# The second condition's norm sums, fifteen products further back in the tensor engine's order

## The chip, the cores and the metric

One core of a Trainium2 chip runs the whole program. The core has TensorE (PE, the matrix engine), VectorE (DVE), ScalarE (ACT), GpSimd (POOL) and SyncE (SP), which here only issues DMAs. Each engine works through its own queue in order; the engines meet at semaphores. The metric is the device time of one execution in microseconds, the median of the runs shown; less is better.

## The reference

The program is a small flow-matching trunk: two layers over 256 latent tokens, with 256 context tokens as a prefix, width 1024. Every layer is a half-step SwiGLU, a token mixer (an mLSTM in the first layer, windowed attention with sinks in the second), and another half-step SwiGLU. Each sub-layer's input is shifted and scaled by vectors made from a condition, and its output goes through a norm:

```python
def modulate(s, m, slot):
    return s * (1 + m[..., 3 * slot + 1, :]) + m[..., 3 * slot, :]

def residual_post_norm(s, y, gate, weight, g, b):
    return layer_norm(ALPHA * s + weight * gate * y, g, b)

for i in range(DEPTH):
    m_l = (lat_cond @ mod_w[i] + mod_b[i])      # condition of the latent tokens
    m_c = (ctx_cond @ mod_w[i] + mod_b[i])      # condition of the context tokens
    h  = residual_post_norm(h,  swiglu(modulate(h,  m_l, 0), ...), gate_of(m_l, 0), 0.5, ...)
    hc = residual_post_norm(hc, swiglu(modulate(hc, m_c, 0), ...), gate_of(m_c, 0), 0.5, ...)
    ...
```

Latent and context tokens share all weights and differ in the condition. The context's last sub-layers are not needed, so the last two norms have latent tokens alone.

## The kernel before

**Layout.** Activations lie with the 1024 features on eight blocks of 128 partitions (`as_[0]` to `as_[7]`, "d" or "t" below) and the 512 tokens in the free dimension. Columns 0 to 255 are the context (`C0`, "context half" below, the first condition), columns 256 to 511 the latent tokens (`C1`, "latent half", the second condition). Matrices are multiplied as sums of three products: each fp32 operand is split into a high part and a low part (h and l: uh, ul; hh, hl), and high x high, high x low and low x high are added. Weights arrive by DMA as `raw`, and are split by ACT (line 413) and DVE (line 414) into `w`.

**The planner.** PE's and SP's order is written by a planner. Every stage is a Python generator, a task; `drive` keeps a clock of estimated time, `k.T`, which every planned product advances, and always takes the due task of the best priority. A task that yields a number asks to be taken up again that many planned nanoseconds later. The table `LAT` on line 32 has five such delays, all used in the class `Norm`. The order of ACT, DVE and POOL is made afterwards by a scheduler that goes by its own estimates, so it can shift when PE's order does.

**A norm with two halves.** Four norms have both halves: behind the first SwiGLU, behind the mLSTM, and behind the next two SwiGLUs ("first" to "fourth norm" below). For each half, in this order:

- The last products of the sub-layer (`y`) end; DVE adds them to the residual (line 830) and the engines sum values and squares over the eight blocks (lines 99 to 108, tiles `acc`, `sq`).
- `Norm.finish` waits a planned delay, `LAT[0]` for the context half and `LAT[1]` for the latent half, and then puts the sums over the partitions into PE's queue: four products on columns and one of 128x256 into the tile `stat` (the profile counts two passes for each).
- ACT takes them out of PSUM (lines 166, 167, 170); POOL makes the inverse root (lines 168, 865 to 870, tile `ln`) and subtracts the mean (line 173, eight times).
- After `LAT[2]` two products spread the inverse root over the partitions (tile `rstd`).
- For each block DVE multiplies by it (line 197); the condition's scale and shift give the next stage's input: uh by ACT (line 624), uf and ul by DVE (lines 625 and 626). The tiles `A` and `B` of the norm are named cA or cB in the profile.
- POOL later scales the residual for the next norm (line 203); `L92` prepares the factors (`ag`) of such a scaling.

After `LAT[3]` or `LAT[4]` the next stage (`g_heads`) may plan its first products: for each half, eight blocks of 12 products of 128x256, so 96 per half (called `xm` before the mLSTM, `gv` before a SwiGLU, `k` and `v` before attention). The context half's 96 products stand in the queue while the latent half's norm is worked on, and the latent half's 96 follow.

```python
        yield LAT[0] if cs == s.halves[0] else LAT[1]      # line 156
        ...                                                # stat products, inverse root
        yield LAT[2]                                       # line 179
        yield from s.scale(cs, y)                          # rstd products, lines 197, 624 to 626
```

**Around the norms.** The conditions' matrices are worked through beside the main stages by `mods`: DMAs of `mraw`, products with a scalar on ACT (line 532) and DVE (line 534) into `macc`, then sums over the partitions (`msum`) and transposes (`mtp`) on PE. These tasks rest while a norm is near: `k.calm` opens `CALM` = 10,000 planned ns after the latent half's sums, and is closed again for `CM` = 80,000 ns when the mixer's first products have been planned (line 995, in `g_ml_main`). `split` gives weight splits another priority while `calm` is closed.

**Start of the mLSTM.** `g_ml_main` plans the `xm` products of the first four of 16 blocks for both halves, then the others with all 512 columns at once. Per block `g_tile` lets DVE copy xm out of PSUM (line 1057), convolve it (lines 1060 and 1061), split it (line 612, `xcl`), and plans products for `v`, `q` and the scores `S`. POOL issues stores of the residual (line 1000, `rs`) between its scalings.

Of the kernel before, what the change touches and what calls it, by code (L numbers as in the profile page):

```python
# [28 lines left out]
MLP, ZP, ATP, HNP, VP = (2,), (1, 3), (2,), (1,), (1, 3)  # L29


LAT = (1700, 3500, 3000, 2000, 2200)

SOLO, RY, ST, LT = 2000, 14000, 2500, 1500

# [37 lines left out]
class Norm:  # L73
# [75 lines left out]
    def finish(s, cs):  # L149
# [5 lines left out]
        k.res[cs.start] = Ev()  # L155
        yield LAT[0] if cs == s.halves[0] else LAT[1]

# [19 lines left out]
        if s.left == 0:  # L177
            k.free(s.a1, s.a2)
        yield LAT[2]
        yield from s.scale(cs, y)  # L180

    def scale(s, cs, y):
# [7 lines left out]
        c = 0 if cs == C1 else 1  # L190
        s.ready[cs.start].t = k.T + (LAT[3] if cs == s.halves[0] else LAT[4])
        y = bc[:, cs]
# [1436 lines left out]
```

## Time and profile before

| | |
|---|---|
| median of 3 runs | 1928.77 us (1927.26 to 1932.07) |
| profiled execution, device time | 1928.09 us |
| its span, first to last instruction | 1926.1 us, 27938 instructions |
| mean granted clock of PE | 0.986 |
| DMA | 287.48 MB, 149 GB/s in the mean |
| first norm: latent sums on PE at | 409.04 us |
| second norm | 835.56 us |
| third norm | 1210.85 us |
| fourth norm | 1586.27 us |

The profile has one execution. A row of the timeline gives the start, the time from the start of the first to the end of the last instruction in the row, engine, line, operation, tiles (written <- read), shape and count; in brackets stands the idle time of the engine before the row and what ended it. A row of the waits gives the sum of such idle times, their number and the longest. All of PE's products are issued by one helper, line 323 (transposes by line 330), so they are told apart by their tiles.

### The profile page before, as it was taken

How to read it: one execution, taken by the hardware profiler on the slowest of the kernel's cores; microseconds unless marked ns; L12 is line 12 of the kernel's file. 1: busy time of each engine (PE TensorE's matmuls, PEld its weight loads, DVE VectorE, ACT ScalarE, POOL GpSimd, SP SyncE). 2: the span in 40 equal slices, each digit the busy share in tenths (PEclk: the TensorE clock that was granted, in tenths of full speed). 3: DMA queues.
4: the chain of work that ended last, by engine and by line, in shares of the span. 5: the costliest groups of instructions: out<-in, count | busy, mean ns of one | idle time of the engine just before them, and what ended most of it. 6: DMA issues, size and time to landing. Idle time of an engine off the chain costs nothing.

```text
span 1926.1 us, 27938 instructions
## 1 busy us (share of the span) xinstructions
PE 1876.3 (97%) x10474; PEld 1587.1 (82%) x10474; DVE 1356.8 (70%) x2489; ACT 829.4 (43%) x1557; POOL 358.1 (19%) x384
## 2 busy tenths in 40 slices
PE   7999999999999999989999999999999999989997
PEld 4888888897879987988888889888888899788887
DVE  4976677976664689777775768877633468977675
ACT  3443233246645564343323333433223335747562
POOL 2000000470012344450000015500000246120000
PEclk9999999999999999989999999999999999999999
DMA  9665455426343464325455443354422323125652
GB/s 319 211 210 170 153 177 179 137 93 204 99 155 103 143 224 143 103 91 183 165 202 175 169 138 131 125 191 165 153 88 93 104 73 132 45 67 178 209 170 100
DMA packets 227432, 287.48 MB, mean 149 GB/s; under 512 B 7969, under 2 KB 197537, under 8 KB 227297
## 3 DMA queue, kind: packets, MB, share of 16 engines
q1 hardware_dynamic: 226384, 282.75, 44.1%
q0 software_dynamic: 912, 2.95, 0.4%
q8 instruction: 82, 1.34, 0.3%
q14 instruction: 54, 0.43, 0.1%
HBM read 269.94 MB, written 15.73 MB: 148 GB/s over the span
## 4 chain that ended last, share of the span: by engine, by line
PE 56%; DVE 3%; POOL 1%; issue 1%; ACT 0%; DVEq 0%; POOLq 0%
PE gv L323 31%; PE y L323 19%; PE q L323 1%; PE s L323 1%; PE o L323 1%; DVE ul L626 1%; PE pT L330 1%; PE stat L323 0%; DVE uf L625 0%; PE msum L323 0%; PE h L323 0%; DVE as L197 0%; POOL as L173 0%; ACT e L1457 0%; PE swap L323 0%
## 5 line engine op out<-in xcount | busy, mean ns | idle before, releaser
L323 PE MATMUL gv<-uh,w 128*128 128x512 f32 (+1 forms) x2240 | 670.3, 381 | 11.0 <-DVE w L414 5.5
L413 ACT ACTIVATE w<-raw 128x512 fp32r<-128x512 f32 x636 | 394.6, 629 | 656.1 <-PE gv L323 357.6
L414 DVE TENSOR_TENSOR w<-raw,w 128x512 fp32r<-128x512 f32 x604 | 432.5, 722 | 270.9 <-ACT w L413 266.1
L323 PEld LDWEIGHTS gv<-uh,w 128*128 128x128 f32 x2240 | 416.2, 190 | 97.3 <-DVE w L414 5.7
L323 PE MATMUL gv<-ul,w 128*128 128x512 f32 (+1 forms) x1120 | 424.5, 379 | 0.1
L534 DVE SCALAR_TENSOR_TENSOR macc<-mraw,cs,macc 128x512 f32<-128x512 f32 x448 | 330.6, 781 | 36.6 <-DMA mraw<-in_mod_w 26.4
L323 PE MATMUL y<-hh,w 128*128 128x512 f32 (+1 forms) x1248 | 340.8, 359 | 0.0
L323 PEld LDWEIGHTS y<-hh,w 128*128 128x128 f32 x1248 | 222.6, 189 | 37.8 <-issue 2.2
L323 PEld LDWEIGHTS gv<-ul,w 128*128 128x128 f32 x1120 | 212.8, 190 | 38.7 <-DVE ul L626 0.6
L323 PE MATMUL y<-hl,w 128*128 128x512 f32 (+1 forms) x624 | 222.4, 356 | 0.0
L88 POOL TENSOR_TENSOR as<-as,shift 128x512 f32<-128x512 f32 (+1 forms) x40 | 57.2, 1463 | 886.2 <-ACT shift L86 886.2
L323 PEld LDWEIGHTS y<-hl,w 128*128 128x128 f32 x624 | 117.9, 189 | 17.5 <-issue 0.7
L323 PE MATMUL gv<-up,w 128*128 128x256 f32 x704 | 124.2, 338 | 1.5 <-ACT up L624 1.2
L323 PEld LDWEIGHTS gv<-up,w 128*128 128x128 f32 x704 | 108.1, 190 | 17.5 <-ACT up L624 1.4
L830 DVE SCALAR_TENSOR_TENSOR as<-y,gate,as 128x256 f32<-128x256 f32 x192 | 82.0, 475 | 37.7 <-PE y L323 37.7
L323 PE MATMUL z<-w,uh 128*128 128x256 f32 x512 | 94.2, 285 | 0.0
L323 PE MATMUL xm<-uh,w 128*128 128x512 f32 (+1 forms) x320 | 91.7, 360 | 0.0
L323 PE MATMUL y<-hnh,w 128*128 128x512 f32 (+1 forms) x320 | 85.0, 350 | 0.0
L414 POOL TENSOR_TENSOR w<-raw,w 128x512 fp32r<-128x512 f32 x32 | 45.7, 1429 | 201.6 <-ACT w L413 193.6
L323 PEld LDWEIGHTS z<-w,uh 128*128 128x128 f32 x512 | 79.9, 192 | 2.5 <-issue 2.1
L743 DVE TENSOR_TENSOR sg<-sg,gv 128x512 f32<-128x512 f32 x66 | 44.9, 684 | 47.7 <-PE gv L323 46.3
L323 PE MATMUL z<-w,ul 128*128 128x256 f32 x256 | 72.4, 283 | 0.0
(318 smaller groups left out, 2519.8 us busy)
## 6 DMA issues: line engine op xcount, KB each, us to landing
raw<-in_ffn_w_in SPq DMA_DIRECT2D x84, 1024.0 KB, 5.2
mraw<-in_mod_w SPq DMA_DIRECT2D x128, 512.0 KB, 6.1
raw<-in_ffn_w_out SPq DMA_DIRECT2D x48, 768.0 KB, 4.6
raw<-in_ml_w_up SPq DMA_DIRECT2D x15, 1024.0 KB, 6.0
m<-in_mod_w SPq DMA_DIRECT2D x32, 256.0 KB, 6.6
raw<-in_ffn_w_out SPq DMA_DIRECT2D x16, 512.0 KB, 3.5
raw<-in_ml_w_down SPq DMA_DIRECT2D x16, 512.0 KB, 4.1
raw<-in_at_w_qkv SPq DMA_DIRECT2D x6, 1024.0 KB, 5.2
```

The costliest lines, as they stand in the source:

```text
L88: nc.gpsimd.tensor_tensor(out=k.as_[d][:, cols], in0=k.as_[d][:, cols], in1=sh[:, cols], op=ALU.subtract)
L323: k.nc.tensor.matmul(out, lhsT=lhsT, rhs=rhs, start=start, stop=stop, skip_group_check=True, **kw)
L330: k.nc.tensor.transpose(out, in_, k.ident[0:p, 0:p])
L413: k.nc.scalar.activation(h, view, AF.Copy)
L414: (k.nc.gpsimd if pool else k.nc.vector).tensor_tensor(out=l, in0=view, in1=h.bitcast(F32), op=ALU.subtract)
L534: V.scalar_tensor_tensor(out=o, in0=r, scalar=cf, in1=o, op0=ALU.mult, op1=ALU.add)
L626: nc.vector.tensor_tensor(out=lo, in0=f[:, cs], in1=hi.bitcast(F32), op=ALU.subtract)
L743: nc.vector.tensor_tensor(out=sg[:, cols], in0=sg[:, cols], in1=gv[1][:, cols], op=ALU.mult)
L830: nc.vector.scalar_tensor_tensor(out=k.as_[d][:, cs], in0=ys[dp][e][:, part], scalar=G[:, d, c:c + 1], in1=k.as_[d][:, cs], op0=ALU.mult, ...
```

## The change

One number of the planner's table: the latent half's sums are planned 5000 instead of 3500 planned ns after the half's last products.

```diff
-LAT = (1700, 3500, 3000, 2000, 2200)
+LAT = (1700, 5000, 3000, 2000, 2200)
```

No instruction is added or removed; their order changes. On PE, at the first norm, the latent half's sums leave their place in the third block's products (`uh_3477`) ...

```order
 L323 MATMUL xm<-ul_3478,w 128x256
-L323 MATMUL xm<-uh_3477,w 128x256
-L323 MATMUL stat<-ones_85,acc_2963 128x1 x2
-L323 MATMUL stat<-ones_85,acc_2964 128x1 x2
-L323 MATMUL stat<-acc_2963,ones_85 128x256
-L323 MATMUL xm<-uh_3477,w 128x256
+L323 MATMUL xm<-uh_3477,w 128x256 x2
 L323 MATMUL xm<-ul_3478,w 128x256
```

... and stand behind the fourth block (`uh_3479`), ahead of the fifth (`uh_3481`):

```order
 L323 MATMUL xm<-ul_3480,w 128x256
 L323 MATMUL xm<-uh_3479,w 128x256
+L323 MATMUL stat<-ones_85,acc_2963 128x1 x2
+L323 MATMUL stat<-ones_85,acc_2964 128x1 x2
+L323 MATMUL stat<-acc_2963,ones_85 128x256
 L323 MATMUL xm<-uh_3481,w 128x256
 L323 MATMUL xm<-ul_3482,w 128x256
```

Of the context half's 96 products 33 stood ahead of the sums and 48 do now; the rstd products follow 30 products later in both, behind 63 and 78. It is so at all four norms (at the fourth 39 became 51, and 69 became 81).

On POOL, at the first norm, the inverse root (line 168 on) stood behind seven of the context half's eight scalings of line 203, and now stands behind all eight:

```order
 L108 TENSOR_TENSOR acc_2964<-acc_2964,sq 128x256 x2
-L203 TENSOR_SCALAR as<-as,ag 128x256 x7
+L203 TENSOR_SCALAR as<-as,ag 128x256 x8
 L168 TENSOR_TENSOR ln<-ln 128x2
 L865 TENSOR_TENSOR ln<-ln,mhalf 128x2
```

The same holds for POOL at the third norm. On PE, at the start of the mLSTM behind the first norm, these are the first products over all 512 columns:

```order
 L323 MATMUL xm<-uh_3473,w 128x512
+L323 MATMUL v<-bv,xm 128x128 x16
 L323 MATMUL xm<-uh_3475,w 128x512
 L323 MATMUL xm<-ul_3476,w 128x512
 L323 MATMUL xm<-uh_3475,w 128x512
-L330 MATMUL mtp<-ident,macc 128x128 x4
 L323 MATMUL xm<-uh_3477,w 128x512
 L323 MATMUL xm<-ul_3478,w 128x512
 L323 MATMUL xm<-uh_3477,w 128x512
-L323 MATMUL v<-bv,xm 128x128 x16
 L323 MATMUL xm<-uh_3479,w 128x512
 L323 MATMUL xm<-ul_3480,w 128x512
```

The v products moved ahead by six wide products, and the transposes of the condition's sums (mtp) are gone from here; the four msum products that stood nine products before the end of the latent half are gone too. Both come again later, msum among the wide products behind the first score products (S). Six wide products (`uh_3481`, `uh_3483`) that stood ahead of the first q product stand behind the first block of S.

On DVE, at the third norm, the condition's products (line 534) come in between the weight splits (line 414) and the latent half's first scaling (line 197). Here the change alone is shown by its + rows; before, the same place had three splits and no row of line 534:

```order
+L626 TENSOR_TENSOR ul_11325<-uf,uh_11324 128x256
+L626 TENSOR_TENSOR ul_11327<-uf,uh_11326 128x256
+L414 TENSOR_TENSOR w<-raw,w 128x512 x2
+L534 SCALAR_TENSOR_TENSOR macc<-mraw,cs,macc 128x512 x4
+L414 TENSOR_TENSOR w<-raw,w 128x512
 L197 TENSOR_TENSOR as<-as,rstd 128x256 x2
 L625 TENSOR_SCALAR uf<-as,cBA,cBB 128x256 x2
```

The four rows of line 534 moved ahead of line 197. At the second norm one row of line 534 moved so on DVE, and four of line 532 on ACT stand between line 170 and the latent half's line 624; SP issues their loads behind the fifth of the raw loads of `ffn_w_in` there, where it was behind the seventh. From each of these places on, tasks that rest on planned times are taken up at other moments, so that rows of the condition's products and of the weight splits change places all through the program.

## The prediction

> **What bounds the kernel now.** First the page's busy times, then what TensorE waited for.
>
> ```profile
> PE 1876.3 (97%) x10474; PEld 1587.1 (82%) x10474; DVE 1356.8 (70%) x2489; ACT 829.4 (43%) x1557; POOL 358.1 (19%) x384
> ...
> PE gv L323 <- DVE w L414: 5.5, 1, 5.5
> PE stat L323 <- DVE acc L107: 4.5, 3, 1.7
> ```
>
> TensorE (PE) is busy for 97% of the span: whatever stands in its queue costs its own time, and a change of order can win only waits. The second wait row is the change's target: three waits of 4.5 us in sum, each in front of the sums of the latent half, the second condition. The largest wait, for split weights in the second norm, is not touched by the table. I then asked for the windows around the first norm and for PE's timeline there.
>
> ```profile
> 406.50:409.63 3.13, 1.45 (x12) 1.18 (x10) 3.11 (x10) 2.23 (x5) 1.50 (x4) 1.00 0.00 0
> 409.63:413.04 3.41, 3.36 (x14) 3.16 (x14) 3.41 (x10) 1.60 (x5) 2.69 (x5) 0.52 0.01 2
> 413.04:416.46 3.42, 3.42 (x17) 3.42 (x17) 3.00 (x6) 0.00 (x0) 3.09 (x6) 0.50 0.51 153
> ...
> 407.08 0.28 PE L323 MATMUL xm<-uh,w 128*128 128x256 f32 x1
> 409.04 1.65 PE L323 MATMUL stat<-ones,acc 128*128 128x1 f32 x8 [1.68 <-DVE acc L107]
> 411.19 0.78 PE L323 MATMUL xm<-uh,w 128*128 128x256 f32 x1
> 417.35 0.61 PE L323 MATMUL rstd<-ident,ln 128*128 128x128 f32 x4
> 417.71 0.36 PE L323 MATMUL xm<-uh,w 128*128 128x256 f32 x1
> 432.06 0.28 PE L323 MATMUL xm<-uh,w 128*128 128x256 f32 x1
> ```
>
> The columns of the windows are length, busy time of PE, weight load, DVE, ACT and POOL, granted clock, DMA. PE idles 1.68 us before the sums, and the granted clock is half (0.52, 0.50) in the next 6.83 us. From 417.71 to 432.06 stand 120 products, the first and the last shown, so one takes 0.12 us. After the rstd product 33 products of the context half are left, then the latent half begins, at 417.71 + 33 x 0.12 = 421.7.
>
> So the price looks like 1.7 us of wait and 3.4 us of half clock. But what decides is when the latent half can begin, which hangs on a chain over the other engines.
>
> ```profile
> 409.23 0.42 DVE L108 TENSOR_TENSOR acc<-acc,sq 128x256 f32<-128x256 f32 x1
> 409.56 0.42 DVE L626 TENSOR_TENSOR ul<-uf,uh 128x256 fp32r<-128x256 f32 x1
> 412.21 0.49 DVE L625 TENSOR_SCALAR uf<-as,cBA,cBB 128x256 f32<-128x256 f32 x1
> ...
> 411.76 0.79 POOL L203 TENSOR_SCALAR as<-as,ag 128x256 f32<-128x256 f32 x1 [0.32 <-DVE uf L625]
> 412.52 0.22 POOL L168 TENSOR_TENSOR ln<-ln 128x2 f32<-128x2 f32 x1
> 415.57 0.53 POOL L870 TENSOR_TENSOR ln<-ln 128x2 f32<-128x2 f32 x1
> ...
> 418.06 0.75 DVE L197 TENSOR_TENSOR as<-as,rstd 128x256 f32<-128x256 f32 x2 [2.02 <-PE rstd L323]
> 420.37 1.83 DVE L626 TENSOR_TENSOR ul<-uf,uh 128x256 fp32r<-128x256 f32 x2
> ```
>
> The chain is: squares summed (L108, done 409.65), sums on PE, inverse root on POOL (L168 to L870, 412.52 to 416.10, 3.58 us), rstd on PE, scaling (L197) and modulation on DVE. Its first ul is done half-way through the last row, at 421.3. PE reaches the latent half at 421.7, so the chain has only 0.4 us of slack: the slow PE stretch runs beside it and hides it. That is the most that a faster PE can win here, unless the chain gets faster too.
>
> **The change, part by part.** In all four norms with two halves the sums and the rstd product move 15 products of the context half back (33 to 48 and 63 to 78 of 96; at the fourth 12); PE's instruction count stays. 18 products instead of 33 are left behind rstd to cover the modulation.
>
> *First norm.* The 33rd product ends at about 407.2; 15 more take 1.8 us, so PE comes to the sums at 409.0, and the wait is gone but for the squares at 409.65. The sums took 409.04 to 411.19 at about half clock, so some 1.1 us at full: done at 410.4. The next 30 products take 3.6 us (their ul is there from 409.98 on, the second L626 row's end for the fifth of eight column blocks), and PE comes to rstd at 414.0. But POOL now has the eighth L203 ahead of L168. It follows the L625 that ends at 412.70, starts 0.17 later as its neighbours do and takes 0.79: 413.66, where L168 stood at 412.52. With the same 3.58 us, L870 ends at 417.24. So rstd runs at 417.3, as before (417.35): **a wait of 3.3 us takes the place of one of 1.7.** Behind it in PE's queue stand the 18 products (to 419.9 at full clock) and the whole latent half; the latter waits for its first ul at 421.3 instead of starting at 421.7. Term: -0.4 us.
>
> *Start of the mixer behind the first norm.* The planner now takes up the gate sums (msum, mtp) much later, and puts the v products behind 3 wide xm products instead of 9.
>
> ```profile
> 432.02 1.58 POOL L203 TENSOR_SCALAR as<-as,ag 128x256 f32<-128x256 f32 x2
> 433.64 0.25 DVE L92 TENSOR_SCALAR ag<-par 128x8 f32<-128x8 f32 x2 [0.99 <-POOL as L203]
> 433.79 0.68 DVE L1057 COPY xm<-xm 128x512 f32<-128x512 f32 x1
> 442.61 0.69 DVE L612 TENSOR_TENSOR xcl<-xc,xch 128x512 fp32r<-128x512 f32 x1
> ...
> 432.27 1.07 PE L323 MATMUL msum<-macc,onew 128*32 128x512 f32 x8
> 434.91 0.62 PE L323 MATMUL xm<-uh,w 128*128 128x512 f32 x2
> 435.83 0.60 PE L330 MATMUL mtp<-ident,macc 128*128 128x128 f32 x4
> 443.35 0.50 PE L323 MATMUL q<-xcl,bm 128*128 128x512 f32 x1 [0.37 <-DVE xcl L612]
> ```
>
> Here DVE's copy of xm (L1057) stands behind L92, and L92 waits for POOL's last L203. POOL's chain starts 1.14 us later; it has one L203 (0.79) less to do there, and one row-store issue more ahead of the last L203 (an estimate of about 0.7), so L92 falls 1.1 us later. From the first L1057 to the end of the first xcl (9.5 us) DVE has as many instructions as before, so xcl and the q product come 1.1 us later, at 444.5. Up to there PE has less to do: the msum (1.0), the mtp (0.35, the time to the next product) and 6 wide products (0.23 apiece, by the start of the second in the row of two) now stand further back, where the waits list shows no idle time: 2.75 us that filled this stretch and now come on top. Term: +3.9 us. From below it is 0, if these pieces fall into later waits and L92 isn't later; from above 3.9 plus a clock window, 5.6.
>
> *Second norm.*
>
> ```profile
> 835.56 1.36 PE L323 MATMUL stat<-ones,acc 128*128 128x1 f32 x8
> 840.88 0.60 PE L323 MATMUL rstd<-ident,ln 128*128 128x128 f32 x4
> ...
> 843.48 1.84 DVE L626 TENSOR_TENSOR ul<-uf,uh 128x256 fp32r<-128x256 f32 x2
> ...
> 834.62 0.37 SPq L420 DMA_DIRECT2D raw<-in_ffn_w_in  x1
> ...
> mraw<-in_mod_w SPq DMA_DIRECT2D x128, 512.0 KB, 6.1
> ```
>
> Here the sums wait for nothing: the 5.5 us for weights lie ahead of them. 15 more products make them 2.1 us late (the first three at half clock), at 837.7; with 1.1 for the sums and 3.6 for 30 products rstd comes at 842.4, 1.5 late. First ul: 844.4 + 1.5 = 845.9. PE went on 0.36 after rstd, as at the first norm, and began the latent half at 841.24 + 4.0 = 845.2. Term: +0.7. ACT gets four gate products (L532) ahead of the latent half's uh, and SP issues their load right behind the raw load at 834.62: landed by about 841.2, four of 0.6 us done at 843.7, while L197 ends its first at about 843.5. I cost that at nothing; if the load comes late, the latent half waits for it.
>
> *Third norm.*
>
> ```profile
> 1218.10 0.36 PE L323 MATMUL gv<-uh,w 128*128 128x256 f32 x1
> ...
> 1215.36 1.89 DVE L414 TENSOR_TENSOR w<-raw,w 128x512 fp32r<-128x512 f32 x3
> 1218.45 0.96 DVE L197 TENSOR_TENSOR as<-as,rstd 128x256 f32<-128x256 f32 x2 [1.20 <-PE rstd L323]
> 1220.47 1.84 DVE L626 TENSOR_TENSOR ul<-uf,uh 128x256 fp32r<-128x256 f32 x2
> 1249.76 2.07 DVE L534 SCALAR_TENSOR_TENSOR macc<-mraw,cs,macc 128x512 f32<-128x512 f32 x3
> ```
>
> DVE now does four gate products (L534, 2.07 / 3 = 0.69 each) between the weight splits and L197: 1217.25 + 2.8 = 1220.0 for L197 instead of 1218.45. First ul 1.55 late, at 1222.95; PE began the latent half at 1218.10 + 4.0 = 1222.1. Term: +0.9; bounds 0 (if the gate products run earlier) and 1.6.
>
> *Fourth norm.*
>
> ```profile
> 1594.29 0.71 PE L323 MATMUL rstd<-ident,ln 128*128 128x128 f32 x4 [0.27 <-POOL ln L870]
> ```
>
> rstd waited for POOL already, whose order isn't changed here: that chain hides the moved products. Term: 0.
>
> *Clock.* Every new wait of over 1 us may bring a half-clock window of 3.41 us, as the windows at 409.63 show after 1.68 us of idle time; one costs 1.7 us where it falls on work that isn't waiting. Bounds 0 and 4 x 1.7 = 6.8; I take one, 1.7, since most would fall on the 18 products that then wait anyway. [...]
>
> Sum: -0.4 + 3.9 + 0.7 + 0.9 + 0 + 1.7 = **+6.8 us**. The profiled execution took 1928.09 us, 0.7 below the median of the runs, 1928.77; on that median the forecast is 1935.5.
>
> **The rivals.** (1) *Faster: the waits vanish and nothing follows.* At the first norm 1.7 of wait and 3.4 of half clock, at the third and fourth the other 2.8 of wait: -7.9, 1920.9 us. For it speak the wait rows; against it that POOL would have to begin L168 by about 410.7, and its order puts it behind the eighth L203. From there it decides: if rstd runs at 414 and not at 417, this rival wins. (2) *The same: the waits change places, and the mixer takes back what its start loses.* The 2.75 us moved back would fall into waits like this one:
>
> ```profile
> PE hT L330 <- DVE zl L1293: 1.6, 2, 1.1
> ```
>
> With -0.4 + 1.1 + 0.7 + 0.9 that is +2.3, 1931.1 us. Against it: those waits come much later, in the heads' stage, and their chains move with PE. (3) *Slower still: half clock after every new wait*, 6.8 in place of 1.7: +11.9, 1940.7. (4) *No new wait costs clock:* each one falls so that the window around it stays busy enough; the sum is 5.1, 1933.9 us, just within no change. For it: the three waits of before are gone, and the new ones are split over two places at each norm; against it the windows at 409.63. [...] That the table moves nothing is excluded: the order of the changed program has the sums 15 products later.
>
> **How the numbers follow.** Forecast (terms as above, 1931 to 1939 by their bounds) 0.52; rival 2 0.23; rival 3 0.13; rival 4 0.05; rival 1 0.07. A measurement of this kernel tells 0.3%, 5.8 us, from no change: above 1934.6 is slower. Of the forecast's 0.52 I put 0.37 above and 0.15 below that. Slower 0.37 + 0.13 = 0.50, the same 0.15 + 0.23 + 0.05 = 0.43, faster 0.07. The range from 1927 to 1941 takes in rivals 2 and 3 and leaves out rival 1 and the ends.
>
> **What would show it.** In the new profile the wait of stat for L107 should be nearly gone and waits of rstd for L870 (about 3 us at the first norm) and of xm, gv and k for ul (1 to 3 us) stand in its place; v should wait for L1057 and q for xcl by 4 us or more in all behind the first norm; L197 of the third norm should follow L534. The prediction is wrong if rstd at the first norm runs more than 1 us earlier against L108 than now, if the mixer's start shows no such waits, or if the difference lies outside the four norms and the mixer's start.

## The result, and the profile after

The changed kernel takes **1949.52 us** (median of 4 runs, 1947.69 to 1951.84), the kernel before 1928.60 (4 runs, 1927.26 to 1932.07): the ratio is 1.0103, with a 95% interval from 1.0087 to 1.0119. It is slower by 20.9 us, three times the forecast of 6.8, and outside its range. The profiled execution of the change took 1951.84 us, its span is 1950.1, 24.0 more than the span of before. One execution of the kernel before beside e9 to e12 below was slow (2318.03 us, at a mean clock of 0.751); it is left out, and the median of the ten others is 1928.37.

The page's busy times, and the list of what TensorE waited for (us in total, times, longest), after the change:

```profile
PE 1884.7 (97%) x10474; PEld 1592.6 (82%) x10474; DVE 1359.4 (70%) x2489; ACT 830.1 (43%) x1557; POOL 365.3 (19%) x384
...
PE rstd L323 <- POOL ln L870: 5.9, 2, 3.6
PE gv L323 <- DVE w L414: 5.8, 2, 5.0
PE gv L323 <- ACT uh L624: 4.8, 2, 3.5
PE h L323 <- ACT vh L611: 3.3, 1, 3.3
PE k L323 <- DVE ul L626: 2.9, 2, 1.8
...
PE h L323 <- DVE rc L1220: 2.4, 1, 2.4
PE S L323 <- DVE ql L612: 2.4, 1, 2.4
...
PE v L323 <- DVE xm L1057: 1.9, 1, 1.9
PE xm L323 <- DVE w L414: 1.3, 1, 1.3
```

The 4.5 us of waits of the sums for L107 are gone from the list. In their place stand the expected waits of rstd, k, v and q (q is in rows left out here), and three kinds that the prediction did not name: h for vh and for rc, and S for ql. PE's busy time rose by 8.4 us, although the number of its instructions is the same.

How far the changed kernel is behind can be read from the starts of the same products in both traces. The first column of numbers has these starts on PE's timeline of before; the others say how much each profile lost in the stage that ends there. "Again" is another execution of the change (e10 below), "before again" another of before (e9); e1 to e6 are experiments. In this section and below, **modulation work** means the condition's products (L532, L534), their sums (msum) and the transposes of these (mtp). The stages hold the same products but for one place: of those that before does ahead of the first S product, the change does msum, mtp and six wide xm products behind it, in the tiles.

| stage ends at | start before | change | again | before again | e1 | e2 | e3 | e4 | e5 | e6 |
|---|---|---|---|---|---|---|---|---|---|---|
| first norm, sums of the latent half | 409.04 | 0.7 | -0.8 | 0.6 | 0.7 | -1.3 | 0.3 | -0.6 | 0.0 | 1.1 |
| first S product (mixer's start) | 449.12 | 3.7 | 3.1 | 0.6 | 4.8 | 0.6 | 3.1 | 3.2 | 5.4 | 0.6 |
| first h product (tiles) | 647.20 | 6.9 | 6.8 | -0.1 | 7.0 | 0.1 | 0.5 | 2.4 | 0.5 | -0.1 |
| first y behind the last h (heads) | 772.95 | 0.8 | 1.6 | 2.7 | 1.0 | 0.3 | 1.6 | 0.5 | 4.1 | 1.9 |
| first y of the second norm's FFN | 968.56 | 3.7 | 3.7 | 1.8 | -0.5 | 3.8 | -0.6 | 2.1 | -0.4 | 0.1 |
| first y of the third norm's FFN | 1346.10 | 3.7 | 2.9 | 0.0 | 0.0 | 3.8 | 0.0 | 0.1 | 1.4 | 0.1 |
| last k of the fourth norm | 1609.21 | 1.8 | 1.8 | 0.0 | 0.0 | 1.7 | 0.0 | 0.1 | -0.1 | 0.1 |
| end of the span | 1926.12 | 2.8 | 0.0 | 1.4 | 1.4 | -0.4 | 1.8 | -1.6 | -0.1 | 1.8 |
| sum | | 24.0 | 19.0 | 7.0 | 14.3 | 8.4 | 6.6 | 6.3 | 10.8 | 5.7 |

The sums are of single executions, so they can stand off from the medians given with each experiment, by 5 to 6 us in e5 and e6. "Before again" is the yardstick: with the same instructions in the same order, one execution loses 2.7 us in the heads, 1.8 at the second norm and 1.4 in the last stage against another. In the heads PE, DVE and ACT have the order of before in e2 to e6 too, and in e8 and e12 below, and yet these lose 0.3 to 5.0 us there: what one profile loses in the heads can't be put down to its order there. What the change does every time is in the rows that agree in both of its columns and in the experiments that have that part: the mixer's start (3 to 4), its tiles (7), the second norm (3.7), the third (3 to 4), the fourth (1.8, but not in e11 below).

**First norm.** PE's timeline of the change (start, busy time, engine, line, operation, names, count, and in brackets the idle time ahead with its releaser):

```profile
409.72 1.26 PE L323 MATMUL stat<-ones,acc 128*128 128x1 f32 x8
...
414.11 0.50 PE L323 MATMUL xm<-uh,w 128*128 128x256 f32 x2 [1.27 <-DVE w L414]
...
418.87 0.71 PE L323 MATMUL rstd<-ident,ln 128*128 128x128 f32 x4 [2.24 <-POOL ln L870]
```

The sums no longer wait. A wait for split weights (L414) is new, and rstd waits for POOL, as forecast. POOL's timeline shows why:

```profile
413.63 1.63 POOL L203 TENSOR_SCALAR as<-as,ag 128x256 f32<-128x256 f32 x1 [0.32 <-DVE uf L625]
415.23 0.62 POOL L168 TENSOR_TENSOR ln<-ln 128x2 f32<-128x2 f32 x1
...
418.62 0.20 POOL L870 TENSOR_TENSOR ln<-ln 128x2 f32<-128x2 f32 x1
```

The eighth L203, which now stands ahead of L168, took 1.63 us; the seventh, ahead of L168 in before, took 0.79. At the start of the mixer, on DVE's timeline:

```profile
436.51 0.24 DVE L92 TENSOR_SCALAR ag<-par 128x8 f32<-128x8 f32 x2 [3.47 <-POOL as L203]
436.67 1.88 DVE L1057 COPY xm<-xm 128x512 f32<-128x512 f32 x3
```

L92 waits for POOL's last L203 and starts 2.87 us later than before (433.64), and the first copy of xm (L1057), which the v products wait for, stands behind it.

**Tiles of the mixer.** DVE's timeline of the change, where S waits for ql (575.36 on PE, idle for 2.38):

```profile
566.20 2.07 DVE L534 SCALAR_TENSOR_TENSOR macc<-mraw,cs,macc 128x512 f32<-128x512 f32 x3
568.18 0.68 DVE L612 TENSOR_TENSOR xcl<-xc,xch 128x512 fp32r<-128x512 f32 x1
568.79 3.78 DVE L534 SCALAR_TENSOR_TENSOR macc<-mraw,cs,macc 128x512 f32<-128x512 f32 x4
...
574.62 0.68 DVE L612 TENSOR_TENSOR ql<-q,qh 128x512 fp32r<-128x512 f32 x1
```

DVE works off eight of the condition's products (L534), bursts of three and four among them, ahead of ql. Before, they stood elsewhere: msum missed its place ahead of the mixer, and all modulation work behind it slid back.

**Second norm.** ACT's timeline of the change:

```profile
853.44 2.56 ACT L532 ACTIVATE macc<-mraw,cs 128x512 f32<-128x512 f32 x4 [2.37 <-DMA mraw<-in_mod_w]
```

DVE's timeline there:

```profile
856.14 0.84 DVE L534 SCALAR_TENSOR_TENSOR macc<-mraw,cs,macc 128x512 f32<-128x512 f32 x1 [7.03 <-DMA mraw<-in_mod_w]
856.91 0.74 DVE L197 TENSOR_TENSOR as<-as,rstd 128x256 f32<-128x256 f32 x2
```

PE's timeline there:

```profile
853.94 0.60 PE L323 MATMUL rstd<-ident,ln 128*128 128x128 f32 x4
...
858.00 0.38 PE L323 MATMUL gv<-uh,w 128*128 128x256 f32 x1 [1.31 <-ACT uh L624]
859.52 0.39 PE L323 MATMUL gv<-ul,w 128*128 128x256 f32 x1 [1.14 <-DVE ul L626]
```

rstd is early enough, but L197 stands in DVE's queue behind one L534, and that waits for its load. SP issues three of them from 847.47 on. ACT's four L532 read the first, and L534 reads the second: it was issued at 848.1, took 8.0 us and landed at 856.1, just when L534 begins. That L534 waits for the load, and not for ACT's L532, can be seen on DVE's timeline of e10, another execution of the change:

```profile
854.79 1.30 DVE L534 SCALAR_TENSOR_TENSOR macc<-mraw,cs,macc 128x512 f32<-128x512 f32 x1 [7.05 <-DMA mraw<-in_mod_w]
```

ACT's timeline of e10 there:

```profile
852.25 2.57 ACT L532 ACTIVATE macc<-mraw,cs 128x512 f32<-128x512 f32 x4 [2.75 <-DMA mraw<-in_mod_w]
```

There L534 begins before the last L532 has ended (854.82), and the second load landed at 854.7. So in the change L197 starts 2.97 us behind rstd; before, it was 0.72 (840.88 to 841.60).

**Third norm.** DVE's timeline of the change:

```profile
1233.42 2.95 DVE L534 SCALAR_TENSOR_TENSOR macc<-mraw,cs,macc 128x512 f32<-128x512 f32 x4
...
1238.98 0.75 DVE L197 TENSOR_TENSOR as<-as,rstd 128x256 f32<-128x256 f32 x2 [2.00 <-POOL as L173]
```

POOL's timeline there:

```profile
1231.01 2.84 POOL L203 TENSOR_SCALAR as<-as,ag 128x256 f32<-128x256 f32 x2 [0.65 <-ACT uh L624]
1233.82 0.63 POOL L168 TENSOR_TENSOR ln<-ln 128x2 f32<-128x2 f32 x1
...
1237.40 0.20 POOL L870 TENSOR_TENSOR ln<-ln 128x2 f32<-128x2 f32 x1
```

PE's row of rstd:

```profile
1237.65 1.22 PE L323 MATMUL rstd<-ident,ln 128*128 128x128 f32 x4 [3.63 <-POOL ln L870]
```

The four L534 stand ahead of L197, as in the order, but DVE is idle for 2.00 us more ahead of L197: that waits for rstd and for L173, which both stand behind L870 on POOL, and there the last two L203 took 1.42 us apiece ahead of L168.

### The profile page after: what moved, and what is told of

Read it like the earlier page. It is cut to its first block, busy times and chain, and to the rows that moved or that the text cites. A ratio compares the mean times of both kernels' runs of the same rounds, so it can differ in the third digit from the quotient of the medians.

```text
span 1950.1 us, 27931 instructions
## 1 busy us (share of the span) xinstructions
PE 1884.7 (97%) x10474; PEld 1592.6 (82%) x10474; DVE 1359.4 (70%) x2489; ACT 830.1 (43%) x1557; POOL 365.3 (19%) x384
## 4 chain that ended last, share of the span: by engine, by line
PE 61%; DVE 3%; POOL 2%; issue 2%; DMA 1%; ACT 1%; SPq 0%; DVEq 0%; POOLq 0%; ACTq 0%
PE gv L323 30%; PE y L323 19%; PE z L323 4%; PE h L323 2%; PE q L323 1%; PE s L323 1%; DMA mraw<-in_mod_w 1%; PE o L323 1%; DVE ul L626 1%; PE k L323 1%; PE msum L323 1%; PE pT L330 1%; PE v L323 1%; DVE uf L625 0%; DVE as L197 0%
## 5 line engine op out<-in xcount | busy, mean ns | idle before, releaser
L414 DVE TENSOR_TENSOR w<-raw,w 128x512 fp32r<-128x512 f32 x604 | 436.1, 728 | 280.5 <-ACT w L413 275.9
L534 DVE SCALAR_TENSOR_TENSOR macc<-mraw,cs,macc 128x512 f32<-128x512 f32 x448 | 331.8, 783 | 51.7 <-DMA mraw<-in_mod_w 48.1
L830 DVE SCALAR_TENSOR_TENSOR as<-y,gate,as 128x256 f32<-128x256 f32 x192 | 82.1, 475 | 38.7 <-PE y L323 38.6
L414 POOL TENSOR_TENSOR w<-raw,w 128x512 fp32r<-128x512 f32 x32 | 45.8, 1433 | 219.4 <-ACT w L413 209.4
```

Of the source, the lines that this page charges most:

```text
L414: (k.nc.gpsimd if pool else k.nc.vector).tensor_tensor(out=l, in0=view, in1=h.bitcast(F32), op=ALU.subtract)
L534: V.scalar_tensor_tensor(out=o, in0=r, scalar=cf, in1=o, op0=ALU.mult, op1=ALU.add)
L830: nc.vector.scalar_tensor_tensor(out=k.as_[d][:, cs], in0=ys[dp][e][:, part], scalar=G[:, d, c:c + 1], in1=k.as_[d][:, cs], op0=ALU.mult, ...
```

## The experiments

**Is the loss one thing or the sum of places?** e1 has 5000 at the first norm alone, e2 at the other three:

```diff
-LAT = (1700, 3500, 3000, 2000, 2200)
+LAT = (1700, (5000, 3500, 3500, 3500), 3000, 2000, 2200)
...
-        yield LAT[0] if cs == s.halves[0] else LAT[1]
+        yield LAT[0] if cs == s.halves[0] else LAT[1][s.n]
```

(s.n counts the norms; e2 has (3500, 5000, 5000, 5000).)

> 5000 at the first norm, 3500 at the other three. Theory A (the loss sits where the plan was moved, and the places add up): the trace of the changed kernel is 11.1 us behind between the first norm and the first h product of the mixer's head phase, so +11 us, about 1939.7. Rival B (most of the loss is one thing common to all stages, such as the slower pace of TensorE in the last stage or a lower clock): +5 us or less, and the products of the last stage again at 236 ns.

> 3500 at the first norm, 5000 at the second, third and fourth. Theory A: second norm 3.7, third 3.7, fourth 1.7 in the trace of the changed kernel, so +9 us, about 1937.7, and with the kernel that has 5000 at the first norm alone it adds up to 19 to 21. Rival B (the later norms only inherit a disturbance of the first): +2 us or less.

Measured against 1930.35 for before: e1 1939.58 us (ratio 1.0045, 1.0029 to 1.0061), e2 1940.39 (1.0049, 1.0037 to 1.0061). That is +9.2 and +10.0, 19.3 in sum against 19.1 to 20.9 for the whole change (e10 and the first measurement). Theory A holds: the places add up, and each column of the table has its loss only where its plan was moved.

**The later sums, or the modulation work that they push aside?** e3 keeps 5000 at the first norm, but shortens the quiet time behind it by the same 1500, so that msum and mtp keep their places ahead of the mixer. e4 is the reverse: the sums where they were, the quiet time longer by 1500.

```diff
-            k.calm.t = k.T + CALM
+            k.calm.t = k.T + (8500, 10000, 10000, 10000)[s.n]
```

(e4: 11500 for 8500, and 3500 at every norm.)

> 5000 at the first norm alone, and the planner's quiet time behind that norm cut from 10000 to 8500, so that the modulation products (msum, mtp) stay ahead of the mixer as before. What is left of the change is the place of the sums and of the reciprocal deviation. Theory A (the later sums themselves cost: waits for the reciprocal deviation, for xm and for q): +4 to +5 us, as the trace of the changed kernel is behind by 4.8 at the mixer's start. Rival C (the displaced modulation products and the order of the tile phase that comes with them are the cost): +1 us or less.

> 3500 everywhere, the quiet time behind the first norm 11500 for 10000: the sums stay where they were, the modulation products miss their place ahead of the mixer and come in its tile phase. Theory A (the later sums themselves cost): within 1 us of before. Rival C (the displaced modulation products cost, by the waits of S for ql and of h for vh in the tile and head phases, 2.4 and 2.0 us): +5 to +6 us.

Measured: e3 1934.07 us (1.0017, 1.0005 to 1.0030), +3.7; e4 1933.57 (1.0018, 1.0005 to 1.0032), +3.2. Neither theory alone: the sums cost 3.7, the displaced modulation work 3.2 without any change of the sums, and both together, e1, 9.2. But e4's loss is not where it was expected: PE waits only 0.5 us for ql and 1.0 for vh in its profile (2.4 and 3.3 in the change). It loses at the mixer's start, where q waits 2.7 us (0.7 in before) and 6.8 us at half clock follow. In the table e3 loses nothing in the tiles (0.5) and e1 7.0. Worked out from the distances of the products' starts in e1, 6.5 of the 7.0 are: msum and mtp themselves 1.3, the six wide xm products 1.4, twelve z products that stand here and no longer in the heads 1.7 (the heads give 1.4 back), and the wait for ql 2.1 (in the change 2.4).

e5 does at all four norms what e3 does at the first, and starts the second layer's modulation stream 4000 of planned time later; TensorE's order then differs from that of before in 87 rows. e6 asks the same for the second norm alone:

```diff
-            k.calm.t = k.T + CALM
+            k.calm.t = k.T + (8500, 8500, 8500, 8500)[s.n]
...
-                k.spawn(k.mod_stream(*todo[1]), 6)
+                k.spawn(k.late(4000, k.mod_stream(*todo[1])), 6)
...
+    def late(k, t, g):
+        yield t
+        yield from g
```

(e5 with 5000 at every norm; e6 with 5000 at the second only and CALM as before.)

> 5000 at all four norms, but the quiet time behind each is 8500 and the modulation stream of the second layer starts 4000 of planned time later, so that the modulation work keeps its places of before: TensorE's order differs from before by 87 lines where the change differs by 2569. Theory C (about half of the loss is the modulation work that the later sums push aside): +8 to +10 us, about 1939, made of 3.7 at the first norm and the mixer's start, 1 at the second norm, 2.5 at the third, 1.5 at the fourth. Theory A (the sums' own waits are all of it): +17 to +20 us, as with the change.

> 5000 at the second norm alone, with the modulation stream of the second layer started 4000 later, so that its first four gate products (L532 on ACT) come behind the latent half's uh as before. Theory C (these gate products cost the 1.3 and 1.1 us of waits for uh and ul and the half clock behind them): TensorE 1 us or less behind at the end of the second norm's stage, in place of 3.7; time +1. Rival (the later sums alone make uh and ul late): 3 us or more behind, time +3 to +4.

Measured against 1931.30: e5 1935.78 us (1.0029, 1.0019 to 1.0040), +4.5; e6 1931.75 (1.0007, 0.9996 to 1.0018), +0.5. So the moved sums by themselves cost 4.5 of the 20.9 us, even less than theory C said, and the other 15 to 16 come with the modulation work (19.1 and 20.9, less 4.5), the half clock behind its waits included. e6 shows it at one place; its waits in the second norm's stage:

```profile
PE gv L323 <- DVE w L414: 5.5, 1, 5.5
PE gv L323 <- DVE as L830: 2.0, 1, 2.0
PE gv L323 <- DVE ul L626: 0.7, 1, 0.7
```

The wait for uh is gone, and the stage loses 0.1 us where the change and e2 lose 3.7 and 3.8.

**Would POOL's order have saved it?** e7 is e5 with POOL's inverse root ahead of the context half's eight L203; e8 does that to the kernel before.

```diff
-        yield RY
+        yield 18000 if cs == s.halves[0] else RY
...
-            nc.gpsimd.tensor_scalar(out=r, ...)
+            k.tc.keep_in_program_order(nc.gpsimd.tensor_scalar(out=r, ...))
```

> As the kernel with the sums alone moved, and on POOL the reciprocal deviation of the latent half (L168 to L870) and L173 stand ahead of the context half's eight L203. Theory P (the waits of rstd for L870, 2.3 us at the first norm and 3.6 at the third, come from the eighth L203 ahead of L168): both waits below 1 us, 3 to 5 us faster than the kernel with the sums alone. Rival (POOL's later L203 then delay L92 and with it L1057 and v at the mixer's start, and the chain over L168 is late anyway): within 1.5 us of it.

> 3500 as before, only POOL's order changed: L168 to L870 and L173 of the latent half ahead of the context half's L203; TensorE's order is that of before. Theory P (the reciprocal deviation's chain over POOL sets when the latent half begins at the first and third norm): 1 to 2 us faster than before, as L168 then starts up to 1 us earlier. Rival (the latent half begins when TensorE comes to it): within 0.5 us of before.

Measured: e7 1948.96 us (1.0086, 1.0071 to 1.0101), 13 slower than e5; e8 1943.46 (1.0063, 1.0043 to 1.0083), 12 slower than before. Theory P falls, and the rival was too mild. POOL's timeline of e7 at the first norm:

```profile
412.86 4.37 POOL L168 TENSOR_TENSOR ln<-ln 128x2 f32<-128x2 f32 x1 [7.24 <-ACT ln L167]
...
418.93 0.20 POOL L870 TENSOR_TENSOR ln<-ln 128x2 f32<-128x2 f32 x1
```

PE's timeline of e8 at the mixer's start:

```profile
442.41 1.11 PE L330 MATMUL mtp<-ident,macc 128*128 128x128 f32 x4 [7.32 <-ACT macc L551]
```

ACT's timeline of e8 there:

```profile
441.18 0.69 ACT L1058 ACTIVATE xc<-xm,par 128x512 f32<-128x512 f32 x1 [9.19 <-DVE xm L1057]
441.77 0.59 ACT L551 ACTIVATE macc<-msum 128x512 f32<-128x512 f32 x1
```

L168 started at once in e7 and then took 4.37 us, so that L870 was done only 0.6 us earlier than in e5 (419.13 and 419.74). And the L203 that now came last held up L92, with it L1057 (by the first rival's chain), behind that L1058 and L551 in ACT's queue, and mtp on PE by 7.3 us. The edit delays the scalings at every norm: of e8's profile 8.3 us are lost at the mixer's start, but 3.7 in the heads and 5.5 in the last stage, where 1.7 is a new wait for L203.

**What belongs to the execution, not to the order.** e9 and e10 are before and the change once more, without any edit.

> The kernel before once more, with its instructions in the same order, for another profiled execution. In the last stage the 512-column products followed each other after 231.5 ns in the first profile of before and after 236.7 ns in that of the change, without any wait (2.8 us in sum). Theory D (the pace is drawn anew in each execution): 230 or 236 ns, whichever; stages before the heads within 1 us of the first profile. Rival E (the pace belongs to the order of the program): 231.5 ns again.

> The changed kernel once more, with its instructions in the same order. Theory D (the pace of the last stage is drawn in each execution): 230, 231.5 or 236.5 ns; the waits of rstd for L870, S for ql and h for vh are there again within 1 us each. Rival E (the pace belongs to the program): 236.7 ns again. Time about 1949.5 by both.

e9 took 1935.19 us (one run; before in the same group 1928.37), e10 1947.43 (1.0091, 1.0073 to 1.0109). PE's groups of instructions in 150 us of the last stage, of before (products, busy us, mean ns, idle time):

```profile
L323 PE MATMUL gv<-up,w 128*128 128x512 f32 (+1 forms) x653 | 113.6, 335 | 0.0
L323 PE MATMUL y<-hp,w 128*128 128x256 f32 x224 | 37.4, 328 | 0.0
```

The same of e9, its window 7 us later for its longer way there:

```profile
L323 PE MATMUL gv<-up,w 128*128 128x512 f32 x637 | 112.9, 340 | 0.0
L323 PE MATMUL y<-hp,w 128*128 128x256 f32 x224 | 38.1, 332 | 0.0
```

Without any idle time the same order gets through 877 products in 150 us once and 861 the next time. In the starts of the 512-column products that is a distance of 231.5 and 236.4 ns, with e10 230.0 where the change first had 236.7: theory D. Nor is it the chip alone: e2, e3 and e4, run on one chip with the same products there, have 230.0, 236.0 and 231.7. So the 2.8 us of the last stage in the first profile of the change are not the change's. Of its other stages all behind the first row came again within 1 us; of the three waits, that of h for vh did not (6.0, first 3.3).

e9 also tells what the half clock behind the sums was worth in the kernel before. At its third norm, the granted clock is the last but two of the numbers, in before:

```profile
1211.00:1216.00 5.00, 4.95 (x27) 4.68 (x28) 5.00 (x14) 1.70 (x5) 3.91 (x6) 0.66 0.00 0
```

The same place in e9, 5.6 us later:

```profile
1216.50:1221.50 5.00, 4.95 (x39) 4.81 (x40) 5.00 (x13) 1.60 (x5) 3.78 (x6) 1.00 0.00 0
```

e9 has no half clock there, and none at the fourth norm; its rstd then waits 1.4 and 1.8 us for L870, and both stages take as long as in before (0.0 in the table). So at these two norms the half clock ran beside the chain over POOL and cost nothing.

**Is it the half clock?** e11 puts dummy products, whose results are not used, into the waits for rstd of the first and third norm.

```diff
-        bc = k.ps("rstd")
+        bc, T = k.ps("rstd"), k.T; [k.mm(bc[:, 0:128], k.ident, k.ident, True, True) for _ in range(0 if s.solo or cs == s.halves[0] else WN[s.n])]; k.T = T
```

(WN = (9, 0, 14, 0).)

> The change, with dummy products of TensorE ahead of the latent half's rstd product: 9 at the first norm, 14 at the third, each about 0.2 us by the rstd rows, inside the waits for L870 of 2.3 and 3.6 us; nothing else moves. Theory H (idle time brings the half clock behind it): the half-clock windows behind the two waits go, 1.7 to 3.4 us each where they slow products that wait for nothing, so -2 to -5 us against the change run again. Rival (the half clock there is hidden, or comes anyway): within 1 us of it.

Measured: 1951.34 us (1945.02 to 1953.24; 1.0104, 1.0081 to 1.0127), against 1947.43 for the change in the same group: 3.9 slower, as neither side expected. The profiled execution is the fastest of the four. A window at the first norm's rstd, of e10 (length; PE, weight load, DVE, ACT, POOL; granted clock; DMA):

```profile
417.50:421.50 4.00, 4.00 (x25) 4.00 (x25) 3.30 (x6) 1.13 (x2) 4.00 (x6) 0.63 0.02 7
```

The same place in e11:

```profile
417.00:427.00 10.00, 8.90 (x71) 8.30 (x71) 8.40 (x18) 3.13 (x6) 9.11 (x16) 1.00 0.18 65
```

The half clock is gone, and PE idles for 1.1 us in that window instead; up to the first S product e11 lost 2.3 us against 3.1 of e10, so at most 0.8 was in the clock. At the third norm the comparison fails: five more L534 came ahead of L197 (4.36 us), so that the expectation that nothing else moves was not met. At the first norm theory H falls: there the half clock ran beside the chain over the other engines.

**A smaller step.** e12 is 4000 at every norm, with the modulation work kept.

```diff
-LAT = (1700, 3500, 3000, 2000, 2200)
+LAT = (1700, (4000, 4000, 4000, 4000), 3000, 2000, 2200)
```

(The quiet time is 9500 and the second stream starts 2000 later.)

> 4000 in place of 3500 at all four norms, a third of the change, with the modulation work kept in its places (quiet time 9500, second stream 2000 later). Theory C (the chain over the other engines sets when the latent half begins, the wait for the sums hides inside it): within 2 us of before. Rival F (the waits of 4.5 us for the sums were time on the path, and a smaller step wins them without the new waits): -2 to -4 us.

Measured: 1938.37 us (1.0046, 1.0032 to 1.0059), +10.0. Rival F falls, and theory C's bound too: a third of the step cost more than the whole of it in e5. By stages its profile loses 1.6, 3.8 (mixer's start), 0.5, 5.0 (heads), -1.1, 1.3, 0.2 and 2.0: the mixer's start and the heads are two thirds of it. At the mixer's start the reason can be read: POOL has the eighth L203 ahead of L168 here too, so L870 is done 9.05 us behind the sums (9.10 in the change, 7.05 in before). A third of the delay brings the whole of POOL's new order. The heads' 5.0 can't be put down to the step, since every engine has the order of before there; 1.6 of it is a half-clock stretch (at 756.5) that e6, with the order of before up to there, has too and e9 has not. Why it costs some 5 us more than e5 in the median is open. None of the kernels was faster than before.

## Why the prediction was too small

The direction was right, and so were the waits that it named at the first norm. **The step that failed is the price of the moved modulation work.** The prediction gave it 2.75 us at the mixer's start and 0.9 at the third norm, and at the second it said "I cost that at nothing": 3.7 in all. With this work kept in its places, e5, the change loses 4.5 of 20.9 us, so 15 to 16 go with it. It was priced by its own length and not by what stands behind it in a queue. The terms one by one, beside the stages of the two profiles:

- *First norm, -0.4.* Right within 0.5. The latent half began 0.06 us later against the sums than before, not 0.4 earlier (421.74 to 422.48, with the sums at 409.04 and 409.72), since the eighth L203 took twice its price. The wait of 1.7 became one of 2.24 and one of 1.27; forecast was 3.3.
- *Mixer's start, +3.9.* With the first norm 3.5 was forecast. Against the sums the first S product came 3.7 later in the change, and 2.7 us of moved work (msum, mtp, six xm products) were still to come: 6.4. The mis-sized term is L92's delay: forecast 1.1, measured 2.2 (2.87 less the 0.68 by which the sums themselves were late). POOL's whole chain was late: its L173 behind the inverse root started at 418.77, in before at 416.05, 2.72 later (2.04 without the 0.68) where the prediction had 1.14, by the L203 that took 1.63. From L92 to the first xcl DVE took 8.98 us (8.97 before), as forecast; from there to the first S product it was 7.96, in e10 7.54, against 6.51 before, the rest of the miss: q waits 1.9 and 2.4 us there, for xch on ACT as well, against 0.7. The waits of v and q together, 3.8 and 4.4, are the 4 us that the prediction named.
- *Tiles and heads, 0.* The wait of S for ql, 2.4 and again 2.2. The prediction followed msum and mtp, not the products of L534 that were planned behind them; e3, which keeps them in their places, has no such wait. The displaced work with the sums moved costs 5.5 in the median (e1 less e3). The heads' new waits for vh and rc (5.7 and 8.4) are no shown cost: the stage loses 0.8 and 1.6, and with the order of before up to 2.7.
- *Second norm, +0.7; measured 3.7.* "I cost that at nothing; if the load comes late, the latent half waits for it": it came late. ACT's four L532 were named, the one L534 behind them and ahead of L197 on DVE was not, nor that it reads a second load, which took 8.0 us where the prediction counted with the page's 6.1. e6, without them ahead of the latent half, loses 0.1.
- *Third norm, +0.9; measured 2.9 and 3.7.* The price was put on DVE's queue ahead of L197. But L197 waited for POOL's chain, where the eighth L203 stands ahead of L168 as at the first norm. The order of the change showed that at both norms, and the prediction used it at the first only. In e5, with the eighth L203 ahead but without the L534, L870 is done 8.35 us behind the sums (9.79 in the change, 6.72 in before) and the stage loses 1.4. What the L534 add is not told apart from the half clock behind rstd, which the change has and e5 has not.
- *Fourth norm, 0; measured 1.8.* k waits 2.9 us for ul (before 0.7). In e5 the same wait (2.6) stands there and the stage loses nothing, so the 1.8 go with a second half-clock window behind it (1618 to 1622, at 0.50), which both profiles of the change and e2 have and e5 has not. e11 settles it: with PE's order of the change there and the same two waits (1.1 and 1.5 us), its profile has no half clock and loses nothing (-0.2).
- *Clock, +1.7.* By the windows of the granted clock, both profiles of the change and e2 have one stretch at 0.50 more than before at the second norm and one more at the fourth; by the distances of the products these cost 1.5 to 1.8 us each. At the first norm the windows hardly count, as e11 shows. A third new one, at the mixer's start (from 437.5 in the change, from 445.9 in e10), is nearly hidden: from the first xcl to the first S product e11, without it, takes 7.54 us like e10, the change 7.96. So two new windows count, 3.3 to 3.6 us, where one was forecast; rival 3 had four, rival 4 none. The one at the second norm, in the change:

```profile
860.50:864.10 3.60, 3.60 (x20) 3.60 (x20) 3.60 (x11) 1.86 (x4) 2.92 (x4) 0.53 0.01 2
```

  It followed PE's idle times of 1.31 and 1.14 us. Such idle times did not bring it every time: in e9 the sums wait as long as in before (4.5 us in three waits, the longest 1.7), and at two of these three norms no half clock follows. What decides it is not shown.
- *Rivals 1 and 2.* Rival 1 needed L168 early; e8 gave it a start without the L203 ahead, and L870 still came 7.0 us behind the sums (408.33 to 415.31; before 7.1). The waits of which rival 2 hoped that they would take the losses back did shrink (hT for zl from 1.6 to 0.4, AT's 1.6 for W went), but those of h grew: 5.7 for vh and rc, against 1.3 for vh before.

The prediction said that it would be wrong if the difference lay outside the norms and the mixer's start. In the two profiles 7.7 and 8.4 us of it lie in the mixer's tiles and heads; 2.7 of that is work that it had counted at the mixer's start, so 5 to 6 us are outside, the heads' share uncertain.

## What to carry to other kernels

In a kernel whose order comes from a planner's clock, a number that delays one step moves every task that is due behind it; list these first, and price each not by its own length but by what is queued behind it on its engine. To find out which part of such a change costs, give the displaced tasks their old places back by their own due times: here that left 4.5 of 20.9 us. And profile the kernel before twice, so that differences of one execution are not put down to the change.

## What the runs showed of the hardware

POOL's instructions took longer beside a run of DVE. At the first norm, where DVE does L626, L414 and L959 (all TENSOR_TENSOR) without a break, POOL's four L203 took 8.15 us in e5 and its L168 of 128x2 elements 4.37 in e7, against 2.78 for another four L203 in e5, 4 us earlier, and 0.22 for L168 before. POOL's timeline of e5:

```profile
405.12 2.78 POOL L203 TENSOR_SCALAR as<-as,ag 128x256 f32<-128x256 f32 x4
409.53 8.15 POOL L203 TENSOR_SCALAR as<-as,ag 128x256 f32<-128x256 f32 x4 [1.63 <-DVE uf L625]
```

DVE's timeline of e5 at the end of its run:

```profile
416.20 0.68 DVE L959 TENSOR_TENSOR bv<-par,cst 128x512 f32<-128x512 f32 x1
```

The same of e7:

```profile
416.50 0.68 DVE L959 TENSOR_TENSOR bv<-par,cst 128x512 f32<-128x512 f32 x1
```

In e5 the last L203 was done at 417.68 (409.53 + 8.15) and DVE's run at 416.88; in e7 L168 was done at 417.23 (412.86 + 4.37) and DVE's run at 417.18. So POOL's small instruction ended 0.05 us behind DVE's run, not after the 0.22 us that it took in before. That one engine waits for the other is the author's reading of these rows: DVE was busy beside the earlier four L203 of e5 too (L626, L197 and L830 from 405.52 on), and no kernel here took DVE's operations away to show it by itself.

Whether POOL takes so long is not decided by the order. Up to this place e1, e3, e10 and the change have the same order on POOL, DVE and ACT; the four L203 take 8.15 us in one go in e1, and go through one by one in the three others (0.8, 0.8, 0.8 and 1.6 us), where DVE's L625 beside them takes up to 0.57 us in place of 0.41. In e1 and e5 L870 is done 10.65 us behind the sums, in the three others 9.0 to 9.1, which is much of what their profiles lose more than e3's at the mixer's start (4.8 and 5.4 against 3.1).

The pace of back-to-back products without waits differs by up to 3% between executions of one order (230.0 to 236.7 ns for a 512-column product in the last stage), and stays the same through the stage: such a product lasts 393 to 394 ns in the mean of each 40 us from 1745 to 1905 in before, and 399 from 1785 on in the change. What sets it was not found.
